# The squares of a conv norm, split in two fp32r parts and summed over channels by fp32r products

## The chip, the cores and the metric

The kernel runs on one core of one Trainium2 chip. The time is that of one execution on the device, in microseconds. It was 463.58 us as a median of three runs (463.23, 463.58 and 464.29).

## What is computed

One residual block of a streaming encoder: an RMSNorm, one input projection (1024 to 4096 columns), a gated linear recurrence (HGRN2, 4 heads of 128 channels) beside a gated short convolution over 512 channels, an output projection, the residual sum and a last RMSNorm. The part that matters here is the norm of the convolution's output, over 8 groups of 64 channels:

```python
def grouped_rmsnorm(x, g, n_groups):
    bsz, s, w = x.shape
    xf = x.astype(jnp.float32).reshape(bsz, s, n_groups, w // n_groups)
    y = xf * lax.rsqrt(jnp.mean(xf * xf, axis=-1, keepdims=True) + EPS)
    return (y.reshape(bsz, s, w) * g.astype(jnp.float32)).astype(x.dtype)
...
    y_b = gate_b * causal_depthwise_conv(gate_c * u, conv_w[l])
    o_b = grouped_rmsnorm(y_b, conv_norm_gain[l], CONV_GROUPS) * jax.nn.silu(z_b)
```

x has 1024 positions of 1024 channels, all in float32.

## The kernel before

Activations lie transposed: channels on the 128 partitions, positions along the free axis, in two halves (hf = 0 and 1) of W = 512 positions. A large product is made of two fp32r parts of each operand (a high part, which is the operand cast to fp32r, and a low part, which is what the cast lost): high by high, high by low and low by high, 128x512 each, on line 60. The cast is made on ACT (L314), the subtraction on DVE (L315).

The input projection goes through 14 pairs of column blocks in turn. Most pairs are seven products of 12 matmuls each, two early ones eight. While these stream through TensorE, the work on the results of earlier pairs is put between them. The order on each engine is the order in which the program writes the instructions; no scheduler moves them. The class Stream writes them: mm issues one large matmul and counts it; at(delay, ...) writes something that many matmuls later; later(delay, ...) does so for small jobs on TensorE, in the order in which they fall due, with at least 7 large matmuls between two of them. A job that is written a little later in the program can therefore change places with another.

The function conv_out(j) handles the convolution's output for channels j (four blocks of 128, so two norm groups each). For either half, on_b multiplies the result by its gate on DVE (L638), squares it on ACT (L639, into the tile b), and lets norm run 44 large matmuls after the bank's arrival (60 for j = 0). norm takes the mean over the 64 channels of a group with TensorE: four fp32 products, one for each 128 positions, with the squares as weights and bones, a 128x2 matrix with 1/64 in the rows of either group, as the moving operand. They go to the small tile pss in PSUM. ACT adds epsilon and moves them to r2 (L605), POOL takes the power -1/2 (L202), TensorE transposes r2 (prr), and the rows go through DRAM and come back spread over 64 partitions each (rs2), with which DVE scales the output (L629).

Three other things share the engines there. The recurrence of head j runs beside it: scores (tile psc: two small matmuls, emptied by ACT L481 and DVE L482) and combine (tile po, emptied by DVE L508 and ACT L510 and L511), as small jobs through the same later. All these small results (pss, prr, psc, po) use one pool of PSUM, psb, of two banks taken in turn, so each must wait until what was in its bank two jobs ago has been emptied. And POOL makes three multiplications for each half of the forget gate (L450, L451, L453), two for the gate of the convolution (L649, L650), and the powers. At the end of the projection POOL takes a power for head 3, scales vo (L543), and makes the last gates (L676), while DVE makes the low parts of the output weights (wol, L756).

Of the kernel before, what the change touches and what calls it, by code (L numbers as in the profile page):

```python
# [9 lines left out]
F32 = mybir.dt.float32  # L10
F32R = mybir.dt.float32r
I32 = mybir.dt.int32
AF = mybir.ActivationFunctionType
ALU = mybir.AluOpType
PSUM = bass.MemoryType.PSUM

P = 128
# [4 lines left out]
W = 512  # L22
NH = 4
# [65 lines left out]
def hybrid_block(ctx: ExitStack, tc: tile.TileContext, xT, x, wv, wpair, wout, cols, fgain, out):  # L89
    nc = tc.nc  # L90
    A, V, G, T = nc.scalar, nc.vector, nc.gpsimd, nc.tensor
# [5 lines left out]
    tmp = ctx.enter_context(tc.tile_pool(name="tmp", bufs=8))  # L97
    qk = ctx.enter_context(tc.tile_pool(name="qk", bufs=2))
    const = ctx.enter_context(tc.tile_pool(name="const", bufs=1))
# [3 lines left out]
    psb = ctx.enter_context(tc.tile_pool(name="psb", bufs=2, space=PSUM))  # L103
    pst = ctx.enter_context(tc.tile_pool(name="pst", bufs=2, space=PSUM))
    ctx.enter_context(tc.manual_schedule(engines={mybir.EngineType.PE, mybir.EngineType.SP, mybir.EngineType.Activation, mybir.EngineType.DVE, mybir.EngineType.Pool}))
    pe = Stream(nc)


    BUFS = {"tmp": 8, "keep": 3, "cn": 3}

    def t512(name, tag="tmp"):
        return tmp.tile([P, W], F32, tag=tag, name=name, bufs=BUFS[tag])

    def bank_a(i, name):
        return psa.tile([P, W], F32, tag=f"ps{i}", name=name)
# [1 line left out]
    def f32(ap):  # L117
        return ap.bitcast(F32)
# [12 lines left out]
    epsc = const.tile([P, 1], F32, name="epsc")  # L131
# [42 lines left out]
    def load_x(hf, k):  # L174
        if hf == 0:
            x0[k] = t512(f"x0_{k}")
        at = x_at(hf, k)
        hi, lo = v_parts(hf, k)
        g = col[:, C_NG + k:C_NG + k + 1]
        nc.sync.dma_start(at, xT[k, :, hf * W:(hf + 1) * W])  # L180
        if hf == 0 and k == 0:
            nc.sync.dma_start(col, cols)
        A.activation(hi, at, AF.Copy, scale=g)
        V.scalar_tensor_tensor(lo, at, g, f32(hi), op0=ALU.mult, op1=ALU.subtract)
# [10 lines left out]
    def half_row_sum(i):  # L195
        t, a = divmod(i, 2)
        xr = t512(f"xr{i}", "keep" if i < 3 else "cn") if i < 6 else qk.tile([P, W], F32, tag="kh", name=f"xr{i}")
        nc.sync.dma_start(xr, x[(4 + t) * P:(5 + t) * P, a * W:(a + 1) * W])
        A.activation(xr, xr, AF.Square, accum_out=(ssy if a else ssx[:, 1])[:, t:t + 1])

    def rsqrt(ap):
        G.tensor_tensor(ap, ap, mhalf[:, :ap.shape[1]], op=ALU.pow)  # L202
# [43 lines left out]
    def v_out(hf, t, p_):  # L246
# [3 lines left out]
    G.memset(mask, 1.0)  # L250
    G.affine_select(out=mask, in_=mask, pattern=[[1, P]], compare_op=ALU.is_ge, fill=0.0, base=0,
                    channel_multiplier=-1)
    bones = const.tile([P, 2], F32, name="bones")
    G.memset(bones, 0.0)
    G.memset(bones[0:64, 0:1], 1.0 / 64)
    G.memset(bones[64:128, 1:2], 1.0 / 64)
    for s_ in scbuf:
        G.memset(s_, 0.0)

# [13 lines left out]
        v_mms(0, pa, k)  # L273


    lbt = const.tile([P, 4, NH], F32, name="lbt")
    l0, l1 = col[:, C_HLB:C_HLB + NH], col[:, C_HLB + NH:C_HLB + 2 * NH]
    V.tensor_tensor(lbt[:, 0], l0, l1, op=ALU.max)
    V.tensor_tensor(lbt[:, 1], l0, lbt[:, 0], op=ALU.subtract)
# [77 lines left out]
    def keep(name, n, ps):  # L357
        kept[n, name] = t512(f"{name}_{n}", "keep")
        A.copy(kept[n, name], ps)
# [34 lines left out]
    def add(out_, ps, t):  # L394
        if t is None:
            A.copy(out_, ps)
        else:
            V.tensor_tensor(out_, ps, t, op=ALU.mult if t is rs1 else ALU.add)
# [150 lines left out]
    def conv_y(j, hf):  # L549
        return mb[:, j, hf * W:(hf + 1) * W]  # L550
# [44 lines left out]
    def conv_out(j):  # L595
        cg = col[:, C_CG + j:C_CG + j + 1]


        def norm(hf, sq):
            nm = f"{j}_{hf}"  # L600
            pss = psb.tile([P, 2, 4], F32, tag="ps", name=f"pss{nm}")
            for t in range(4):
                T.matmul(pss[:, :, t], sq[:, t * P:(t + 1) * P], bones, start=True, stop=True)
            r2 = sm.tile([P, 2, 4], F32, tag="r2", name=f"r2{nm}")
            pe.at(3, lambda: A.activation(r2, pss, AF.Identity, bias=epsc, scale=1.0))  # L605
            pe.at(10, lambda: rsqrt(r2.rearrange("p g t -> p (g t)")))

            def to_rows():
                prr = psb.tile([2 * 4, P], F32, tag="ps", name=f"prr{nm}")
                T.transpose(prr, r2.rearrange("p g t -> p (g t)"), ident)  # L610
                rr = sm.tile([2 * 4, P], F32, tag="rr", name=f"rr{nm}", bufs=1)
                pe.at(2, lambda: A.copy(rr, prr))
                pe.at(9, lambda: store(rr))

            def store(rr):
                rows = dram.tile([2 * 4, P], F32, tag="rows", name=f"rows{nm}")
                nc.sync.dma_start(rows, rr)
                pe.at(22, lambda: load(rows))

            def load(rows):  # L620
                rs2 = t512(f"rs2{nm}", "cn")
                for g in range(2):
                    nc.sync.dma_start(rs2[g * 64:(g + 1) * 64, :],
                                      rows[g * 4:(g + 1) * 4].rearrange("t p -> (t p)").partition_broadcast(64))
                pe.at(28, lambda: scale(rs2))

            def scale(rs2):
                y = conv_y(j, hf)
                V.scalar_tensor_tensor(y, y, cg, rs2, op0=ALU.mult, op1=ALU.mult)  # L629

            pe.later(28, to_rows)

        def on_b(hf):
            def on(ps, t):
                y = conv_y(j, hf)
                b = t512(f"b{j}_{hf}", "cn")
                add(b, ps, t)
                pe.at(4, lambda: V.tensor_tensor(y, y, b, op=ALU.mult))  # L638
                pe.at(14, lambda: A.activation(b, y, AF.Square))  # L639
                pe.later(60 if j == 0 else 44, lambda: norm(hf, b))  # L640
            return on

        def on_z(hf):
            def on(ps, t):
                y = conv_y(j, hf)
                z, sg = t512(f"z{j}_{hf}"), t512(f"sg{j}_{hf}")
                add(z, ps, t)
                pe.at(9, lambda: A.activation(sg, z, AF.Sigmoid))
                pe.at(14, lambda: G.tensor_tensor(z, z, sg, op=ALU.mult))  # L649
                pe.at(20, lambda: G.tensor_tensor(y, y, z, op=ALU.mult))  # L650
            return on

        return on_b(0), on_z(0), on_z(1), on_b(1)
# [109 lines left out]
    for g, (n, step) in enumerate(products):  # L763
        if n == npair - 1:
            i = ORDER.index(step)
# [62 lines left out]
    for i, (n, g) in enumerate(jobs):  # L828

        last = i == len(jobs) - 1  # L830
        for c0, c1 in [(0, W // 2), (W // 2, W)] if last else [(0, W)]:
            ps = []
# [21 lines left out]
        t = g[0]  # L854
# [74 lines left out]
```

## Time and profile before

| what | value |
|---|---|
| median of three runs | 463.58 us |
| the profiled execution | 464.61 us, of which 462.9 us are the span of the trace |
| TensorE (PE) | 454.9 us busy, 98% of the span |
| DVE | 326.1 us busy, 70% |
| ACT | 230.4 us busy, 50% |
| POOL | 101.3 us busy, 22% |
| mean granted clock of TensorE | 0.997 |

The span is the time that the profiler saw the engines at work; the device's time lies 1.7 us above it. A share of the busy time says how much an engine did, not whether the others waited for it; where one stands near 100%, only its own work and its waits count.

### The profile page before, as it was taken

What the parts mean: (1) busy time and instruction counts of PE and PEld (TensorE: products, weight loads), DVE (VectorE), ACT (ScalarE), POOL (GpSimd) and SP (SyncE); (2) the same over time, 40 slices, a digit from 0 to 9 for tenths busy, and PEclk for the clock granted to TensorE, in tenths of its full rate; (3) what the DMA queues carried; (4) which work ended last, traced back from release to release, by engine and by line L of the source; (5) the groups of instructions that cost most, each with busy time, mean ns of one, the idle gap of its engine ahead of it and who ended that gap; (6) DMA issues with size and microseconds to landing.
All of it is one profiled execution on the core that took longest, in us unless ns stands there. A gap on an engine that the chain in (4) does not pass through costs nothing. (4 is left out here: it accounts for less than half of the span.)

```text
span 462.9 us, 6245 instructions
## 1 busy us (share of the span) xinstructions
PE 454.9 (98%) x2200; PEld 380.5 (82%) x2200; DVE 326.1 (70%) x593; ACT 230.4 (50%) x553; POOL 101.3 (22%) x92
## 2 busy tenths in 40 slices
PE   8999999999999999999999999999999999999995
PEld 6888888888888887888888888888888888888884
DVE  3658787989977789658799468798466795523333
ACT  5877416474454554454443545454636734314333
POOL 1100000005520053410326210326332443220000
PEclk9999999999999999999999999999999999999998
DMA  8990311020022120022020212020014238101442
GB/s 265 396 380 6 92 45 47 23 68 25 23 92 92 24 68 25 23 92 91 24 69 24 66 49 92 23 90 26 24 33 144 75 101 274 57 2 70 161 157 91
DMA packets 22031, 40.83 MB, mean 88 GB/s; under 512 B 2736, under 2 KB 2800, under 8 KB 22000
## 3 DMA queue, kind: packets, MB, share of 16 engines
q1 hardware_dynamic: 22000, 40.43, 26.3%
q8 instruction: 17, 0.28, 0.2%
q14 instruction: 14, 0.11, 0.1%
HBM read 36.19 MB, written 4.23 MB: 87 GB/s over the span
## 5 line engine op out<-in xcount | busy, mean ns | idle before, releaser
L315 DVE TENSOR_TENSOR lT<-T,hT 128x512 fp32r<-128x512 f32 x48 | 32.5, 678 | 32.4 <-ACT hT L314 32.2
L450 POOL TENSOR_TENSOR kh<-kh,ei 128x512 f32<-128x512 f32 x8 | 11.7, 1465 | 136.5 <-DVE ei L449 136.5
L60 PE MATMUL pb<-XH,lT 128*128 128x512 f32 x96 | 38.9, 405 | 0.0
L60 PE MATMUL pb<-XL,hT 128*128 128x512 f32 x96 | 38.4, 400 | 0.0
L60 PE MATMUL pb<-XH,hT 128*128 128x512 f32 x96 | 37.7, 393 | 0.0
L510 ACT COPY vo<-po 128x128 f32<-128x128 f32 x32 | 8.5, 266 | 53.9 <-DVE st L508 40.4
L314 ACT CAST hB<-B 128x512 fp32r<-128x512 f32 x44 | 27.6, 629 | 10.7 <-issue 10.7
L60 PE MATMUL po<-XH,XL 128*128 128x512 f32 (+1 forms) x88 | 32.6, 371 | 0.0
L60 PE MATMUL po<-XH 128*128 128x512 f32 (+1 forms) x88 | 32.6, 371 | 0.0
L60 PE MATMUL po<-XL,XH 128*128 128x512 f32 (+1 forms) x88 | 32.6, 370 | 0.0
L315 DVE TENSOR_TENSOR lB<-B,hB 128x512 fp32r<-128x512 f32 x44 | 32.3, 733 | 0.2 <-ACT hB L314 0.2
L314 ACT CAST hT<-T 128x512 fp32r<-128x512 f32 x48 | 28.4, 591 | 4.2 <-DVE T L306 4.2
L449 DVE RECIPROCAL ei<-e 128x128 f32<-128x128 f32 x32 | 29.5, 932 | 0.0
L60 PE MATMUL p<-XH,hB 128*128 128x512 f32 x64 | 24.9, 389 | 0.0
L60 PE MATMUL p<-XL,hB 128*128 128x512 f32 x64 | 24.9, 389 | 0.0
L60 PE MATMUL p<-XH,lB 128*128 128x512 f32 x64 | 24.9, 389 | 0.0
L482 DVE COPY_PREDICATED sc<-mask,psc 128x128 f32<-128x128 int32 x32 | 9.6, 300 | 16.7 <-ACT kt L481 16.6
L60 PEld LDWEIGHTS pb<-XL,hT 128*128 128x128 f32 x96 | 18.0, 188 | 4.1
L60 PEld LDWEIGHTS pb<-XH,hT 128*128 128x128 f32 x96 | 18.0, 188 | 3.7
L60 PEld LDWEIGHTS pb<-XH,lT 128*128 128x128 f32 x96 | 18.1, 189 | 3.0
L845 DVE TENSOR_TENSOR r<-po,xo 128x512 f32<-128x512 f32 (+1 forms) x9 | 5.7, 633 | 19.9 <-PE po L60 19.9
L60 PE MATMUL pe<-XL,hT 128*128 128x512 f32 x48 | 19.5, 405 | 0.0
(217 smaller groups left out, 1364.2 us busy)
## 6 DMA issues: line engine op xcount, KB each, us to landing
B<-wpair SPq DMA_DIRECT2D x56, 256.0 KB, 2.7
wo<-wout SPq DMA_DIRECT2D x16, 256.0 KB, 3.0
xo<-x SPq DMA_DIRECT2D x16, 256.0 KB, 3.3
out<-y SPq DMA_DIRECT2D x16, 256.0 KB, 2.3
wv<-wv SPq DMA_DIRECT2D x8, 256.0 KB, 7.5
x<-xT SPq DMA_DIRECT2D x8, 256.0 KB, 5.8
vo<-x SPq DMA_DIRECT2D x4, 512.0 KB
mb<-xT SPq DMA_DIRECT2D x8, 256.0 KB, 6.0
```

The costliest lines, as they stand in the source:

```text
L60: self.T.matmul(*args, **kw)
L314: A.copy(hi, src)
L315: pe.at(5, lambda: V.tensor_tensor(lo, src, f32(hi), op=ALU.subtract))
L449: pe.at(9 + gap * i, lambda c0=i * P: V.reciprocal(eis[0][:, c0:c0 + P], e[:, c0:c0 + P]))
L450: pe.at(10 + 4 * gap - 3, lambda: G.tensor_tensor(kh, kh, eis[0], op=ALU.mult), lambda: G.tensor_tensor(ev[:, :, 0, :], ev[:, :, 0, :], ei ...
L482: lambda: V.copy_predicated(scbuf[(h * NT + pr) % NS], mask.bitcast(I32), psc[:, 0]))
L510: A.copy(vp, po[:, 0])
L845: V.tensor_tensor(r, po[:, c0:c1], xr[:, c0:c1], op=ALU.add)
```

## The change

The squares b are no longer used as fp32. Behind the square ACT casts them to fp32r (sh, the high part), and five large matmuls later in the program DVE subtracts this from b (sl, the low part, rounded to fp32r). bones becomes fp32r (its values 0 and 1/64 are exact), made from a small fp32 tile. norm multiplies either part by bones and sums them in PSUM: eight fp32r products in place of four fp32 ones. pss changes its layout, so that the two columns of a product lie side by side, and r2 is written through a rearranged view. norm comes 4 large matmuls later than before. sh and sl are two more tiles of the ring tmp, of 8 buffers.

```diff
-    bones = const.tile([P, 2], F32, name="bones")
-    G.memset(bones, 0.0)
-    G.memset(bones[0:64, 0:1], 1.0 / 64)
-    G.memset(bones[64:128, 1:2], 1.0 / 64)
+    bones = const.tile([P, 2], F32R, name="bones")
+    lbt = const.tile([P, 4, NH], F32, name="lbt")
+    ones2 = lbt[:, 3, 0:2]
+    G.memset(ones2, 0.0)
+    G.memset(ones2[0:64, 0:1], 1.0 / 64)
+    G.memset(ones2[64:128, 1:2], 1.0 / 64)
+    V.tensor_copy(bones, ones2)
...
-        def norm(hf, sq):
+        def norm(hf, parts):
             nm = f"{j}_{hf}"
-            pss = psb.tile([P, 2, 4], F32, tag="ps", name=f"pss{nm}")
+            pss = psb.tile([P, 4, 2], F32, tag="ps", name=f"pss{nm}")
             for t in range(4):
-                T.matmul(pss[:, :, t], sq[:, t * P:(t + 1) * P], bones, start=True, stop=True)
+                for i, sq in enumerate(parts):
+                    T.matmul(pss[:, t], sq[:, t * P:(t + 1) * P], bones, start=(i == 0), stop=(i == 1))
             r2 = sm.tile([P, 2, 4], F32, tag="r2", name=f"r2{nm}")
-            pe.at(3, lambda: A.activation(r2, pss, AF.Identity, bias=epsc, scale=1.0))
+            pe.at(3, lambda: A.activation(r2.rearrange("p g t -> p t g"), pss, AF.Identity, bias=epsc, scale=1.0))
...
                 pe.at(4, lambda: V.tensor_tensor(y, y, b, op=ALU.mult))
-                pe.at(14, lambda: A.activation(b, y, AF.Square))
-                pe.later(60 if j == 0 else 44, lambda: norm(hf, b))
+                parts = []
+
+                def square():
+                    A.activation(b, y, AF.Square)
+                    parts.extend([t512(f"s{i}{j}_{hf}", dtype=F32R) for i in "hl"])
+                    A.copy(parts[0], b)
+                    pe.at(5, lambda: V.tensor_tensor(parts[1], b, f32(parts[0]), op=ALU.subtract))
+
+                pe.at(14, square)
+                pe.later(64 if j == 0 else 48, lambda: norm(hf, parts))
```

What this does to the order of the instructions is seen at four places. In these rows a name is that of a tile with a running number, which differs between the two programs, and the line numbers of the changed kernel are higher by 2 to 11.

On DVE, at the first norm (j = 0, hf = 0), before the change: the multiplication by the gate (L638), the last of the four reciprocals, and the low parts of the next two weights.

```order
L638 TENSOR_TENSOR mb<-mb,b_0_983 128x512
L449 RECIPROCAL ei_0_966<-e_0_942 128x128
L315 TENSOR_TENSOR lT_3_1011<-T_3_985,hT_3_1010 128x512
L315 TENSOR_TENSOR lB_3_1018<-B_3_861,hB_3_1017 128x512
L398 TENSOR_TENSOR z_0_1030<-pd_923,u_2_1005 128x512
```

And with it:

```order
L641 TENSOR_TENSOR mb<-mb,b_0_984 128x512
L451 RECIPROCAL ei_0_967<-e_0_943 128x128
L648 TENSOR_TENSOR sl_0_1012<-b_0_984,sh_0_1011 128x512
L317 TENSOR_TENSOR lT_3_1015<-T_3_986,hT_3_1014 128x512
L317 TENSOR_TENSOR lB_3_1022<-B_3_862,hB_3_1021 128x512
L400 TENSOR_TENSOR z_0_1035<-pd_924,u_2_1006 128x512
```

The subtraction stands between the reciprocal and the low parts, which move behind it.

On ACT, at the second square of j = 0 (b_1), which is also where r2 of the first norm is made, before:

```order
L359 COPY m_3_1122<-pb_1094 128x512
L639 ACTIVATE b_1_1092<-mb 128x512
L314 CAST hT_3_1131<-T_3_1095 128x512
L605 ACTIVATE r_0_1121<-pss_0_1116,epsc 128x8
L359 COPY m_3_1155<-pd_1124 128x512
L314 CAST hT_3_1160<-T_3_1125 128x512
```

And with the change:

```order
L361 COPY m_3_1121<-pb_1099 128x512
L645 ACTIVATE b_1_1097<-mb 128x512
L647 CAST sh_1_1130<-b_1_1097 128x512
L316 CAST hT_3_1133<-T_3_1100 128x512
L608 ACTIVATE r_0_1149<-pss_0_1140,epsc 128x4x2
L361 COPY m_3_1167<-pd_1123 128x512
L316 CAST hT_3_1172<-T_3_1124 128x512
```

The cast sh_1 stands between the square and what came after it; r2 keeps its place among the others.

On TensorE, at the first norm of j = 1, before: the norm (pss_0), seven large matmuls, and the first combine of head 1 (po_0).

```order
L60 MATMUL pb_1590<-XL,hT_5_1652 128x512
L603 MATMUL pss_0_1779<-bones,b_0_1676 128x2 x4
L60 MATMUL pb_1590<-XH,lT_5_1653 128x512
...
L60 MATMUL pb_1796<-XH,lB_6_1664 128x512
L492 MATMUL po_0_1802<-vo,kt_0_1730 128x128
L495 MATMUL po_0_1802<-vo,sc_97 128x128
```

And with the change:

```order
L60 MATMUL pb_1607<-XH,hT_5_1668 128x512
L494 MATMUL po_0_1802<-vo,kt_0_1751 128x128
L497 MATMUL po_0_1802<-vo,sc_97 128x128
L60 MATMUL pb_1607<-XL,hT_5_1668 128x512
...
L60 MATMUL pb_1818<-XL,hB_6_1680 128x512
L606 MATMUL pss_0_1829<-bones,sh_0_1717 128x2
L606 MATMUL pss_0_1829<-bones,sl_0_1718 128x2
```

The two have changed places; j = 2 and j = 3 do the same, j = 0 doesn't (there the norm and everything small behind it come 4 large matmuls later, but for the two scores products after the norm).

On ACT, at the end of the projection, before: the last result of head 3 (po_7) is copied to vo and squared, and then a bank is copied (m_13).

```order
L510 COPY vo<-po_7_3595 128x128
L511 ACTIVATE po_7_3595,ssa<-po_7_3595 128x128
L359 COPY m_13_3602<-pe_3579 128x512
L755 CAST woh_3573<-wo_7_3575 128x512
L755 CAST XH<-wo_2_3577 128x512
L538 ACTIVATE ssa<-ssa,epsc 128x8
```

And with the change:

```order
L361 COPY m_13_3665<-pe_3644 128x512
L512 COPY vo<-po_7_3661 128x128
L513 ACTIVATE po_7_3661,ssa<-po_7_3661 128x128
L766 CAST woh_3638<-wo_7_3640 128x512
L766 CAST XH<-wo_2_3642 128x512
L540 ACTIVATE ssa<-ssa,epsc 128x8
```

The copy m_13 stands ahead of the two on po_7. On POOL the second scaling of vo then comes after the last two gates instead of before them.

## Rows read from the trace of the kernel before

**Rows 1.** Windows: busy us and instructions of PE, PEld, DVE, ACT, POOL; clock.

```profile
core 0: us, PE busy (x) PEld busy (x) DVE busy (x) ACT busy (x) POOL busy (x), PEclk, DMA share, GB/s
100.00:380.00 280.00, 279.69 (x1412) 234.54 (x1411) 221.09 (x411) 143.20 (x380) 86.25 (x68) 1.00 0.19 59
111.20:120.30 9.10, 9.10 (x45) 7.65 (x44) 9.10 (x17) 4.22 (x9) 5.15 (x5) 1.00 0.00 0
```

**Rows 2.** Timeline of PE at the first norm: start, duration, instruction, idle before.

```profile
117.11 0.39 PE L60 MATMUL pb<-XH,lB 128*128 128x512 f32 x1
117.34 0.95 PE L603 MATMUL pss<-bones,b 128*128 128x2 f32 x8
118.14 0.49 PE L60 MATMUL pd<-XH,hT 128*128 128x512 f32 x1
118.47 0.40 PE L60 MATMUL pd<-XL,hT 128*128 128x512 f32 x1
```

**Rows 3.** Groups of instructions, line 603, TensorE: busy us, mean ns, idle before.

```profile
L603 PE MATMUL pss<-bones,b 128*128 128x2 f32 x64 | 7.7, 242 | 0.3 <-DVE sc L482 0.3
```

**Rows 4.** Timelines of PE and DVE at the first norm of j = 1.

```profile
181.68 0.39 PE L60 MATMUL pb<-XL,hT 128*128 128x512 f32 x1
182.37 1.05 PE L603 MATMUL pss<-bones,b 128*128 128x2 f32 x8 [0.31 <-DVE sc L482]
...
182.02 0.65 DVE L482 COPY_PREDICATED sc<-mask,psc 128x128 f32<-128x128 int32 x2
```

**Rows 5.** Timeline of PE, the last two products of 256 columns.

```profile
456.74 0.28 PE L60 MATMUL po<-XL,XH 128*128 128x256 f32 x1
456.86 0.28 PE L60 MATMUL po<-XH,XL 128*128 128x256 f32 x1
```

**Rows 6.** Groups of instructions, by form: a cast, a subtraction.

```profile
L315 DVE TENSOR_TENSOR lB<-B,hB 128x512 fp32r<-128x512 f32 x44 | 32.3, 733 | 0.2 <-ACT hB L314 0.2
...
L314 ACT CAST hB<-B 128x512 fp32r<-128x512 f32 x44 | 27.6, 629 | 10.7 <-issue 10.7
```

**Rows 7.** Timelines of POOL and DVE, j = 0.

```profile
109.33 1.29 POOL L450 TENSOR_TENSOR kh<-kh,ei 128x512 f32<-128x512 f32 x1 [67.10 <-DVE ei L449]
111.61 0.61 POOL L453 TENSOR_TENSOR kh<-kh,gt 128x256 f32<-128x256 f32 x1
...
110.11 1.06 DVE L315 TENSOR_TENSOR lB<-B,hB 128x512 fp32r<-128x512 f32 x1
120.35 0.62 DVE L638 TENSOR_TENSOR mb<-mb,b 128x512 f32<-128x512 f32 x1
```

**Rows 8.** Timeline of ACT, j = 0: both squares, and r2 of the first norm.

```profile
108.36 0.63 ACT L639 ACTIVATE b<-mb 128x512 f32<-128x512 f32 x1 [1.12 <-DVE mb L638]
...
121.01 0.63 ACT L639 ACTIVATE b<-mb 128x512 f32<-128x512 f32 x1 [1.50 <-DVE mb L638]
...
122.01 0.27 ACT L605 ACTIVATE r<-pss,epsc 128x8 f32<-128x8 f32 x1
```

**Rows 9.** Timeline of PE, the second scores product of head 0.

```profile
123.19 0.38 PE L478 MATMUL psc<-qh,kh 128*128 128x128 f32 x2
```

**Rows 10.** Timelines of POOL, DVE and PE around the second square of j = 1.

```profile
191.09 1.29 POOL L650 TENSOR_TENSOR mb<-mb,z 128x512 f32<-128x512 f32 x1 [0.23 <-POOL z L649]
...
192.07 0.34 DVE L508 SCALAR_TENSOR_TENSOR st<-po,gg,dec 128x128 f32<-128x128 f32 x1
...
193.48 0.39 PE L478 MATMUL psc<-qh,kh 128*128 128x128 f32 x2
```

**Rows 11.** Timelines of ACT, POOL, DVE and PE at the output projection's start.

```profile
365.07 0.59 ACT L359 COPY m<-pe 128x512 f32<-128x512 f32 x1
...
366.97 2.02 POOL L202 TENSOR_TENSOR ssa<-ssa,mhalf 128x8 f32<-128x8 f32 x1 [1.45 <-ACT ssa L538]
...
371.52 3.43 POOL L676 TENSOR_TENSOR za<-za,sga 128x512 f32<-128x512 f32 x2
...
373.74 1.77 DVE L756 TENSOR_TENSOR wol<-wo,woh 128x512 fp32r<-128x512 f32 x1
...
375.59 0.47 PE L60 MATMUL po<-wol,XH 128*128 128x512 f32 x1
```

More of the change, by code (lines that the diff above doesn't have):

```diff
@@ L109, in hybrid_block, with t512 @@
     BUFS = {"tmp": 8, "keep": 3, "cn": 3}
-    def t512(name, tag="tmp"):
-        return tmp.tile([P, W], F32, tag=tag, name=name, bufs=BUFS[tag])
+    def t512(name, tag="tmp", dtype=F32):
+        return tmp.tile([P, W], dtype, tag=tag, name=name, bufs=BUFS[tag])
     def bank_a(i, name):
@@ L273, in hybrid_block @@
         v_mms(0, pa, k)
-    lbt = const.tile([P, 4, NH], F32, name="lbt")
     l0, l1 = col[:, C_HLB:C_HLB + NH], col[:, C_HLB + NH:C_HLB + 2 * NH]
```

## The prediction

> **What bounds the kernel now.** I read the windows first, because they say which engine the end of the program hangs on. In the stretch from 100 to 380 us, where all the squares and norms lie, TensorE is busy 279.69 of 280.00 us, at a granted clock of 1.00 (the upper of the two levels, 2.4 GHz) [rows 1]. Nothing that DVE, ACT or POOL do costs time there unless TensorE must wait for it. So the change is worth two things: the difference in TensorE's own work, and the stalls that it makes or removes. The second number of [rows 1] matters as much: from 111.2 to 120.3 us DVE is busy 9.10 of 9.10 us. There a DVE operation more moves all DVE work behind it.
>
> Next, the timeline of TensorE around one norm, for its price. The products of 128x512 start 0.23 us apart (the last one ahead of the norm at 117.11, the norm at 117.34); the norm's four fp32 products stand as eight passes, from 117.34 to 118.14, that is 0.80 us or 0.10 each, and the fp32r product after them has its successor 0.33 later (118.47) instead of 0.23 [rows 2]. With those 0.10 the norm takes 0.90 us of TensorE's time, 0.112 per pass. For the whole kernel the grouped line has 64 passes for 8 norms of 4 products, so one fp32 product is two passes [rows 3].
>
> Last, I went along TensorE's timeline for places where it does wait. There is one of weight: at 182.37, after the product of 181.68, so 0.69 us later instead of 0.23; the row names DVE's L482, whose two copies run from 182.02 for 0.65 us [rows 4]. They empty the psb bank that the norm wants.
>
> **TensorE's own work.** Removed: 32 fp32 products, 64 passes [rows 3]. Added: 64 fp32r products of the same 128 columns of weights and the same 2 moving columns. No row shows an fp32r product of 2 columns, so I bound it. Two columns by themselves are nothing (0.23 us for 512 columns is 0.001 for two), so what a pass costs is its weights. An fp32r load of 128 columns that isn't hidden costs the 0.10 us by which the product after the norm is late [rows 2]: 64 x (0.10 - 0.112) = -0.8 us. From above, fp32r products of 256 columns start 0.12 us apart [rows 5]: 64 x (0.12 - 0.112) = +0.5. Both ends say that one load is paid per pass, and there are 64 before and after. I take 0.112, a change of 0.
>
> A page of the Trainium skill speaks to this: FP8 and Floating Point Precision, section TensorE Precision Notes, says that true FP32 takes four passes. By it the old norms would be 128 passes, 64 more than the new ones, worth an estimated 64 x 0.112 = 7.2 us. The trace counts two per product, so I don't follow it.
>
> **DVE's and ACT's added work.** Per norm, ACT makes one cast from fp32 to fp32r and DVE one subtraction, both 128x512. The same forms take 0.629 and 0.733 us on the mean [rows 6]; in a row of such work the next one starts some 0.55 us (ACT) and 0.6 us (DVE) later. 8 x 0.6 = 5 us on either engine, which is free as long as it isn't late for TensorE.
>
> It becomes dear where POOL works at the same time. The trace shows it at 110.11: DVE's lB<-B,hB, both operands in SBUF, takes 1.06 us instead of some 0.65, and ends at 111.17; POOL's L450 ran from 109.33 to 110.62 [rows 7]. It ends 0.55 us after POOL is done, as if it had begun only then. The Trainium skill gives a rule for it (SBUF — State Buffer, section Who interferes with whom): a DVE instruction with two SBUF inputs and a GpSimd instruction that reads SBUF exclude each other. The trace agrees with 1.06 us, and it speaks against this change, whose subtraction is of that kind.
>
> **First term, j = 0 (109 to 125 us).** sh_0 stands on ACT right after the square that starts at 108.36 and lasts 0.63 [rows 8]; it ends at about 109.6. The subtraction sl_0 stands on DVE before lT and lB, so it starts inside POOL's L450 and takes over lB's fate: it ends at about 111.17. Then lT, and lB starts at about 111.7, where POOL's L453 runs from 111.61 to 112.22 [rows 7]: lB ends at 112.77 instead of 111.17. DVE is 1.6 us late (1.15 if lB comes first; 0.6 to 0.7 if POOL doesn't get in the way), and without a gap up to 120.3 [rows 1] it stays late until the multiplication L638 of hf = 1, 120.35 in the trace [rows 7]. Its square starts at 121.01 + 1.6 = 122.6; behind it ACT has sh_1 (+0.55), a cast, and then r2 of hf = 0, now done at 122.28 [rows 8]: at 122.28 + 1.6 + 0.55 = 124.4. That r2 empties the bank that the second scores product takes at 123.19 [rows 9]. TensorE is there no later than before, so it waits about 124.4 + 0.1 - 123.2 = 1.3 us. Bounds: with DVE late by 0.65 it waits 0.4; if the blocking goes further, 1.9. I take 1.3.
>
> **Second term, j = 1.** The norm's delay of 48 lets the first combine (po1_0) go ahead of the norm, so po1_0 now wants the bank that L482 empties, at the product where the norm wanted it. The subtraction sl stands ahead of L482 on DVE: 182.67 + 0.7 = 183.4 at most, and DVE can make up some 0.3 to 0.4 by its pauses; the stall of 0.46 [rows 4] grows by about 0.25 (0 to 0.7). For hf = 1, sl_1 would run at about 191.5, inside POOL's L650 (191.09 to 192.38), and ends at 192.9; lT and the state update of 192.07 come after it, so at about 193.6, and ACT's square that empties po1_1 half a microsecond behind at 194.4. The norm's transposes prr want that bank just after the scores of 193.48, at about 194.2 [rows 10]. With the next combine waiting for the state: +0.4 (0 to 0.8). Together +0.65.
>
> **Third term, j = 2 and 3.** The same swap of norm and combine, with the same extra DVE operation, in a stretch with less DVE work. I take +0.1 each (0 to 0.3).
>
> **Fourth term, the start of the output projection.** At 375.59 the product takes wol<-wo, which DVE finishes at 375.51 (L756, 373.74 and 1.77 us: blocked by POOL's L676, two from 371.52 for 3.43, end 374.95, plus 0.55). That POOL chain begins with the pow at 366.97, which waited for ACT [rows 11]. In the changed kernel ACT has the bank copy m (0.59 us, [rows 11]) ahead of the last copy and square of po3_7, so the sum for head 3 comes 0.45 us later, and one step after another so do the pow, the scalings, the gates and wol. TensorE has no slack there: +0.4 (0 to 0.5).
>
> **What costs nothing.** The fp32r ones are made by POOL and DVE before the first product needs DVE. The 16 tiles more in the tmp ring are each free well before they are wanted. ACT's r2 writes the same 8 values per partition in another order. The row loads from DRAM move behind a few weight fetches on SP's queue, but the scaling that waits for them comes some 10 us later; if that cover were gone, the put of the output projection would be late, far behind.
>
> **Sum.** 0 + 1.3 + 0.65 + 0.2 + 0.4 = +2.6 us. The profiled execution took 464.61 us, 1.0 above the median of 463.58 (span 462.9), so by its own time 467.2; against the median 466.2.
>
> **The rivals.** Hidden (chance 0.21): POOL doesn't block sl_0, and DVE's lateness is eaten by pauses and by operations that wait for POOL in any case. Then j = 0 gives 0.4, the rest 0 to 0.4: 463.6 to 464.4. For it: an operation blocked already loses nothing by coming later; against it: [rows 1] has no gap in DVE. Below 464.5 it counts as no change.
>
> Faster (0.06): an fp32r load hides behind the pass before it where an fp32 one doesn't, so a pass costs far less. At half, 64 x 0.056 = 3.6 us saved, 463.58 - 3.6 + 2.6 = 462.6; fully hidden 7.2, so 459.0, or 456.4 without stalls. It decides once a pass costs under about 0.06 us. Against it: the 0.10 of the fp32r product behind the norm [rows 2] is just such a load, not hidden. A third of this chance (0.02) is for old products of four passes each, of which the trace records two: then 64 passes of 128 fall away, again 64 x 0.112 = 7.2 us, 459.0 with the stalls. That is what the rule of four passes (the Trainium skill, FP8 and Floating Point Precision, TensorE Precision Notes) would do here; 64 rows for 32 products [rows 3] speak against it.
>
> Worse (0.08): j = 2 and 3 stall like j = 1, and the blocking in j = 0 goes one operation further: 1.9 + 1.3 + 1.0 + 0.5 = 4.7, 468.3.
>
> **How the numbers follow.** The forecast, slower by the four stalls, has 0.65: 464.6 to 467.6 by its bounds. With the hidden rival's upper part the range is 463.6 to 467.6; it leaves out 0.06 (faster), the worst case of 0.08 and little else. A difference of 0.2% (0.93 us, about as much as the three runs differ) can't be told from none: faster 0.06, same 0.21, slower 0.73.
>
> **What the changed profile would show.** Right: L606 with 64 rows some 0.1 us apart; sl_0 of j = 0 at about 109.6 with 1.5 us; r2 of hf = 0 at about 124; a gap on TensorE before the second scores product of over 1 us, one before po1_0 of 0.5 to 0.9, one of 0.3 to 0.5 at the first wol1. Wrong: no gap before 125 us (then the cover held), or norms that take half of 0.90 us (then the load was hidden). TensorE's busy time should not change by over 0.8 us.

## The result: 1.3% slower, with most of the stalls where the prediction took almost none

The changed kernel takes 469.73 us (median; 469.43 to 470.87), the kernel before 463.4 us beside it: a ratio of 1.0125, 95% interval 1.0101 to 1.0148. The forecast was 466.2 us, 463.6 to 467.6. The direction was right; the size, 2.6 us, was well under half of the 6.3 us that came.

TensorE has the same work and more waits. The windows of the changed kernel give the stretch in which [rows 1] showed 279.69 us busy of 280:

```profile
core 0: us, PE busy (x) PEld busy (x) DVE busy (x) ACT busy (x) POOL busy (x), PEclk, DMA share, GB/s
100.00:380.00 280.00, 276.04 (x1383) 229.24 (x1381) 228.69 (x411) 145.74 (x382) 89.06 (x68) 1.00 0.17 54
```

To see where they lie, I set the start of each 128x512 product of line 60 in one trace against that of the same product in the trace of before, and took the growth of the difference over each stage (products 440 to 700 hold the norms of j = 0, 700 to 800 and 940 to 1070 and 1200 to 1340 those of j = 1, 2 and 3, 1400 to 1460 the first output weights; elsewhere it is 0.05 or less). That leaves the first microseconds out, and they must be left out: in the profiled execution of the changed kernel TensorE is 1.26 us early already at the 20th product, so its span is 4.8 us longer (467.7 against 462.9) where the loss behind that product is 6.1.

| us lost by TensorE | j = 0 | j = 1 | j = 2 | j = 3 | output | all |
|---|---|---|---|---|---|---|
| predicted | 1.3 | 0.65 | 0.1 | 0.1 | 0.4 | 2.6 |
| changed kernel | 1.53 | 0.40 | 1.81 | 1.88 | 0.45 | 6.1 |

The price of a pass was right. The timeline of TensorE at the first norm, which answers to [rows 2]:

```profile
116.76 0.39 PE L60 MATMUL pd<-XH,hT 128*128 128x512 f32 x1
116.99 0.17 PE L606 MATMUL pss<-bones,sh 128*128 128x2 f32 x1
117.02 0.25 PE L606 MATMUL pss<-bones,sl 128*128 128x2 f32 x1
117.13 0.25 PE L606 MATMUL pss<-bones,sh 128*128 128x2 f32 x1
...
117.69 0.25 PE L606 MATMUL pss<-bones,sl 128*128 128x2 f32 x1
117.80 0.49 PE L60 MATMUL pd<-XL,hT 128*128 128x512 f32 x1
118.12 0.40 PE L60 MATMUL pd<-XH,lT 128*128 128x512 f32 x1
```

There are eight passes, the first two 0.03 us apart and the others 0.11. From the first to the product behind them it is 0.81 us, and 0.32 for that product: the 0.80 and 0.33 of before.

At j = 0 the chain came as forecast. The timelines of POOL, DVE, ACT and TensorE, for [rows 7 to 9]:

```profile
108.07 1.30 POOL L452 TENSOR_TENSOR kh<-kh,ei 128x512 f32<-128x512 f32 x1 [67.11 <-DVE ei L451]
...
108.42 1.49 DVE L648 TENSOR_TENSOR sl<-b,sh 128x512 fp32r<-128x512 f32 x1 [0.50 <-ACT sh L647]
...
120.70 0.66 DVE L641 TENSOR_TENSOR mb<-mb,b 128x512 f32<-128x512 f32 x1
...
123.11 0.28 ACT L608 ACTIVATE r<-pss,epsc 128x8 f32<-128x8 f32 x1
...
121.69 0.39 PE L60 MATMUL pa<-XL,hB 128*128 128x512 f32 x1
123.44 0.49 PE L480 MATMUL psc<-qh,kh 128*128 128x128 f32 x2 [1.36 <-ACT r L608]
```

sl_0 takes 1.49 us inside POOL's L452 and ends 0.54 us after it; the multiplication of the next half starts at 120.70, which with the head start of 1.26 is 1.61 us later than in [rows 7] (forecast: 1.6); r2 is done at 123.39, and the scores product waits for it.

The large losses are at j = 2 and 3, with three stalls each. The same engines at j = 2:

```profile
253.33 1.62 POOL L661 TENSOR_TENSOR mb<-mb,z 128x512 f32<-128x512 f32 x1
257.05 1.29 POOL L660 TENSOR_TENSOR z<-z,sg 128x512 f32<-128x512 f32 x1 [2.10 <-ACT sg L659]
...
260.35 1.27 POOL L661 TENSOR_TENSOR mb<-mb,z 128x512 f32<-128x512 f32 x1
...
253.73 1.24 DVE L501 TENSOR_TENSOR gg<-gt 128x3 f32<-128x3 f32 x1
255.08 0.35 DVE L508 TENSOR_SCALAR st<-po,gg 128x128 f32<-128x128 f32 x1
...
257.13 1.75 DVE L641 TENSOR_TENSOR mb<-mb,b 128x512 f32<-128x512 f32 x1
...
260.94 0.30 DVE L484 COPY_PREDICATED sc<-mask,psc 128x128 f32<-128x128 int32 x1 [1.45 <-ACT kt L483]
261.15 1.01 DVE L648 TENSOR_TENSOR sl<-b,sh 128x512 fp32r<-128x512 f32 x1
262.09 0.68 DVE L317 TENSOR_TENSOR lT<-T,hT 128x512 fp32r<-128x512 f32 x1
262.69 0.33 DVE L510 SCALAR_TENSOR_TENSOR st<-po,gg,dec 128x128 f32<-128x128 f32 x1
...
255.82 0.19 ACT L513 ACTIVATION_READ_ACCUMULATOR po<-po 128x1 f32 x1
...
258.92 0.63 ACT L645 ACTIVATE b<-mb 128x512 f32<-128x512 f32 x1 [1.47 <-DVE mb L641]
259.64 0.62 ACT L647 CAST sh<-b 128x512 fp32r<-128x512 f32 x1
...
256.06 0.49 PE L480 MATMUL psc<-qh,kh 128*128 128x128 f32 x2 [0.33 <-DVE z L400]
...
261.30 0.49 PE L480 MATMUL psc<-qh,kh 128*128 128x128 f32 x2 [0.52 <-DVE sc L484]
...
263.70 0.27 PE L613 MATMUL prr<-ident,r 128*8 128x128 f32 x1 [0.18 <-issue]
```

Three DVE operations with both operands in SBUF start while a POOL multiplication of 128x512 runs, and each ends after it: gg (three columns) takes 1.24 us, the multiplication L641 takes 1.75, sl_1 takes 1.01. In the trace of before gg takes 0.15 and the multiplication 0.68. POOL isn't idle there either, but it runs the power L202, of 8 columns, and neither of them is held by that:

```profile
253.24 1.63 POOL L202 TENSOR_TENSOR r<-r,mhalf 128x8 f32<-128x8 f32 x1
...
253.84 0.68 DVE L638 TENSOR_TENSOR mb<-mb,b 128x512 f32<-128x512 f32 x1
254.44 0.15 DVE L499 TENSOR_TENSOR gg<-gt 128x3 f32<-128x3 f32 x1
```

In the changed kernel each of the three holds the bank that the next small job on TensorE wants. gg holds the state update st, and behind that ACT's copies of po, the last of which ends at 256.01; the scores product comes at 256.06 (the row names DVE's z, which that product doesn't read). L641 holds ACT's square, and behind it the casts sh and hT and the copy of kt, for which L484 waited; the product follows at 261.30. sl_1 holds the second st and ACT's copies; prr comes at 263.70.

The output projection starts as forecast: wol ends at 380.31 and TensorE takes it at 380.37, 0.63 after the product before.

```profile
379.74 0.39 PE L60 MATMUL po<-woh,XH 128*128 128x512 f32 x1
380.37 0.50 PE L60 MATMUL po<-wol,XH 128*128 128x512 f32 x1 [0.24 <-DVE wol L767]
...
378.79 1.52 DVE L767 TENSOR_TENSOR wol<-wo,woh 128x512 fp32r<-128x512 f32 x1
```

### The profile page after: what moved, and what is told of

Its sections match the earlier page's. It is cut to its first block, busy times and chain, and to the rows that moved or that the text cites. A ratio compares the mean times of both kernels' runs of the same rounds, so it can differ in the third digit from the quotient of the medians.

```text
span 467.7 us, 6246 instructions
## 1 busy us (share of the span) xinstructions
PE 455.7 (97%) x2200; PEld 378.4 (81%) x2200; DVE 339.6 (73%) x602; ACT 235.9 (50%) x561; POOL 104.1 (22%) x92
## 5 line engine op out<-in xcount | busy, mean ns | idle before, releaser
L452 POOL TENSOR_TENSOR kh<-kh,ei 128x512 f32<-128x512 f32 x8 | 11.7, 1468 | 132.5 <-DVE ei L451 120.3
L316 ACT CAST hB<-B 128x512 fp32r<-128x512 f32 x44 | 27.6, 629 | 10.7 <-issue 10.7
L484 DVE COPY_PREDICATED sc<-mask,psc 128x128 f32<-128x128 int32 x32 | 9.5, 298 | 23.1 <-ACT kt L483 23.0
L202 POOL TENSOR_TENSOR r<-r,mhalf 128x8 f32<-128x8 f32 x8 | 15.3, 1912 | 24.6 <-ACT r L608 24.6
```

What stands on the lines that cost most here:

```text
L316: A.copy(hi, src)
L452: pe.at(10 + 4 * gap - 3, lambda: G.tensor_tensor(kh, kh, eis[0], op=ALU.mult), lambda: G.tensor_tensor(ev[:, :, 0, :], ev[:, :, 0, :], ei ...
L484: lambda: V.copy_predicated(scbuf[(h * NT + pr) % NS], mask.bitcast(I32), psc[:, 0]))
```

## The experiments

Two theories stood at first. Theory 1: the new order does it, since norm and combine have changed places at j = 1 to 3. Theory 2: DVE and ACT have one operation more per norm and are late, whatever the order. The runs have their rows in the table at the end of this section. The kernel before, run beside them, had medians of 464.4, 464.67 and 463.45 us in the three groups of runs, so I go by ratios and by TensorE's loss.

**e1_order_back** keeps the split and gives the norm its old place:

```diff
-                pe.later(64 if j == 0 else 48, lambda: norm(hf, parts))
+                pe.later(60 if j == 0 else 44, lambda: norm(hf, parts))
```

> The changed kernel with the norm's old delays (44, and 60 for j = 0), so that norm and combine stand on TensorE in the order of before; the split and the eight fp32r products stay. Theory 1 (order): most of j = 2 and j = 3 (1.8 us each in the changed kernel) comes from the swap of norm and combine, which moves the gate product gg and the state update on DVE to a place where POOL works; then j = 2 and 3 lose at most 0.3 us each here, the output projection about 0, j = 0 still 1.5, j = 1 0.2 to 0.7: 465.2 to 466.0 us. Theory 2 (load): DVE and ACT have one operation more per norm and are late whatever the order; then j = 2 and 3 still lose 1.2 us or more each: 468 us or more.

Measured: 471.94 us, a ratio of 1.0137 (1.0088 to 1.0187), TensorE 6.4 us late: 1.93, 1.80, 1.41 and 1.13 at the four norms, 0 at the output projection. Theory 1 is wrong on the norms and right on the output projection; the 1.2 us or more of theory 2 came at j = 2 and nearly at j = 3. In the old order gg isn't held (0.15 us), but sl_1 is; at j = 2:

```profile
263.19 1.30 POOL L661 TENSOR_TENSOR mb<-mb,z 128x512 f32<-128x512 f32 x1 [0.23 <-POOL z L660]
...
263.80 1.24 DVE L648 TENSOR_TENSOR sl<-b,sh 128x512 fp32r<-128x512 f32 x1 [0.93 <-ACT sh L647]
...
265.56 0.34 DVE L510 SCALAR_TENSOR_TENSOR st<-po,gg,dec 128x128 f32<-128x128 f32 x1
...
266.53 0.49 PE L480 MATMUL psc<-qh,kh 128*128 128x128 f32 x2 [0.80 <-ACT po L513]
```

One held operation ahead of st, and the scores product waits for po's bank.

**e2_order_only** gives the kernel before the new delays and nothing else:

```diff
-                pe.later(60 if j == 0 else 44, lambda: norm(hf, b))
+                pe.later(64 if j == 0 else 48, lambda: norm(hf, b))
```

> The kernel before with the norm's new delays (48, and 64 for j = 0), fp32 products and no split. Theory 1 (order): j = 2 and 3 lose 1.0 to 1.8 us each by the new order alone, the output projection 0.4, j = 0 nothing, j = 1 gains its old stall of 0.46 and loses as much: 466 to 467.5 us. Theory 2 (load): no stall in j = 2 and 3 over 0.3 us; 463.0 to 464.0 us.

Measured: a ratio of 0.9982 (0.996 to 1.0004). The order alone costs 0 at j = 2 and 3, as theory 2 had it. It wins 0.56 at j = 1, which is the old stall of [rows 4]: the large products around that norm stand 1.61 us apart, those around the other norms 1.04. And it costs 0.43 at the output projection. And yet gg and L638 are held here just as long as in the changed kernel:

```profile
250.00 1.60 POOL L650 TENSOR_TENSOR mb<-mb,z 128x512 f32<-128x512 f32 x1
...
250.39 1.23 DVE L499 TENSOR_TENSOR gg<-gt 128x3 f32<-128x3 f32 x1
...
253.78 1.76 DVE L638 TENSOR_TENSOR mb<-mb,b 128x512 f32<-128x512 f32 x1
...
253.34 0.39 PE L478 MATMUL psc<-qh,kh 128*128 128x128 f32 x2
```

The difference is when. Here gg starts 2.95 us ahead of the scores product, in the changed kernel 1.8 ahead of when it was due (256.06 less the stall of 0.50, less 253.73). In the changed kernel it is 2.33 us from gg's start (253.73) to the product that takes the freed bank (256.06), 1.1 of them the lock. That fits into 2.95 and not into 1.83; the 0.50 by which it doesn't is the stall.

**e3_no_sl** leaves out the subtraction and uses sh twice:

```diff
-                    parts.extend([t512(f"s{i}{j}_{hf}", dtype=F32R) for i in "hl"])
+                    parts.extend([t512(f"sh{j}_{hf}", dtype=F32R)] * 2)
                     A.copy(parts[0], b)
-                    pe.at(5, lambda: V.tensor_tensor(parts[1], b, f32(parts[0]), op=ALU.subtract))
```

> The changed kernel without the subtraction on DVE: the second product of each pair takes sh again, so the output leaves out the low part and counts the high part twice. The cast on ACT and the new order stay. Theory 1 (order): j = 0 loses under 0.5 us (no operation there any more that POOL can block), j = 2 and 3 still 1.0 us or more each: 465.5 to 467.5 us. Theory 2 (load): the DVE operation is the cause everywhere, 463.5 to 464.5 us.

Measured: 2.6 us of loss (0.47, -0.23, 1.14, 0.82 and 0.41), a ratio of 1.0057 (1.0033 to 1.0081). Without any subtraction more than half of j = 2 is still there: the cast alone, in the new order, is enough to be late. At j = 2 gg starts 2.0 us ahead of when the scores product is due, the product comes 2.33 us after it again (252.91 and 255.24), and that is 0.32 late. So neither theory is whole.

**e4_gg_early** is the changed kernel with one tiny operation moved:

```diff
                   lambda: V.copy_predicated(scbuf[(h * NT + pr) % NS], mask.bitcast(I32), psc[:, 0]))
+            if pr == 0:
+                pe.at(2, lambda: V.tensor_tensor(gg[:, 0:3], gts[:, 0:3, 1], gts[:, 1:4, 0], op=ALU.mult))
...
-                if pr == 0:
-                    V.tensor_tensor(gg[:, 0:3], gts[:, 0:3, 1], gts[:, 1:4, 0], op=ALU.mult)
```

> The changed kernel with the small gate product gg of the first half made right after the first scores' copy on DVE in place of ahead of the first state update. If the first link of the chain in j = 2 and 3 is gg, held by POOL's L661 for 1.1 us there (1.24 us in the changed kernel, 0.15 in the kernel before), then the first of the three stalls in j = 2 and in j = 3 (0.50 and 0.57 us) goes, and the blocked multiplication L641 behind it may too: 466.5 to 468.8 us. If gg is only where the blocking shows and another operation takes its place, the loss stays at 1.5 us or more each: 469 to 470 us.

Measured: the loss falls from 6.1 to 2.1 us, j = 2 and 3 from 1.81 and 1.88 to 0.48 and 0.18, more than expected; a ratio of 1.0025 (1.0005 to 1.0046). At its new place gg takes 0.45 us, and the later links hold no one up for long, though L641 and sl are held as before (1055 and 948 ns on the mean).

**e5_j0_late** moves one subtraction past POOL's work:

```diff
-                    pe.at(5, lambda: V.tensor_tensor(parts[1], b, f32(parts[0]), op=ALU.subtract))
+                    pe.at(30 if j == 0 and hf == 0 else 5, lambda: V.tensor_tensor(parts[1], b, f32(parts[0]), op=ALU.subtract))
```

> The changed kernel with one subtraction moved: sl_0 of j = 0, hf = 0 is written 30 large matmuls after the cast in place of 5, past POOL's five multiplications; everything else stays, so DVE does the same work. Theory 1 (POOL's lock): the j = 0 loss of 1.54 us falls to 0.3 to 0.7 us, what 0.6 us of DVE and 0.55 us of ACT leave beyond the slack of 0.9; the other stages stay as in the changed kernel. Theory 2 (mere load): DVE is as full as before, the loss at j = 0 stays at 1.2 to 1.6 us.

Measured: j = 0 loses 1.10 us in place of 1.53, between both expectations, and the rest stays; the ratio is 1.0099 (1.0065 to 1.0132). The reason for the miss is in DVE's next row:

```profile
108.34 0.69 DVE L317 TENSOR_TENSOR lT<-T,hT 128x512 fp32r<-128x512 f32 x1 [0.98 <-ACT hT L316]
```

In the trace of before this lT waited 0.32 us for ACT's hT; now sh stands ahead of hT and lT waits 0.98. The cast alone makes DVE late by 0.58 (the start of L641 in e3_no_sl, 120.73, plus that trace's head start of 0.20, less 120.35); the subtraction itself adds 0.6 (119.71 + 1.82 in this run, 1.18 late); the rest of the 1.61, 0.43, goes with sl_0's place inside POOL's work.

**e8_no_gate** takes POOL's L661 away:

```diff
                 pe.at(14, lambda: G.tensor_tensor(z, z, sg, op=ALU.mult))
-                pe.at(20, lambda: G.tensor_tensor(y, y, z, op=ALU.mult))
```

> The changed kernel without POOL's L661, the multiplication of the convolution's output by its gate (the output leaves that factor out); DVE, ACT and TensorE keep all their work and order. Theory 1 (POOL's lock): gg takes 0.15 us and sl_1 0.7, and j = 2 and j = 3, 1.8 us each in the changed kernel, lose 0 to 0.7 us each. Theory 2 (mere load of DVE and ACT): each loses 1.2 us or more still.

Measured: j = 2 and 3 lose 0.38 and 0.08, as theory 1 (here POOL's lock) had it; all stages lose 0.84, a ratio of 1.001 (0.9988 to 1.0031). The same place as above:

```profile
253.54 0.15 DVE L501 TENSOR_TENSOR gg<-gt 128x3 f32<-128x3 f32 x1
253.79 0.35 DVE L508 TENSOR_SCALAR st<-po,gg 128x128 f32<-128x128 f32 x1
...
259.88 0.68 DVE L648 TENSOR_TENSOR sl<-b,sh 128x512 fp32r<-128x512 f32 x1
...
255.39 0.39 PE L480 MATMUL psc<-qh,kh 128*128 128x128 f32 x2
```

gg starts as late as in the changed kernel (1.85 us ahead of the scores product) and takes 0.15 us; sl_1 takes 0.68. DVE and ACT do all their work, late as it is, and TensorE doesn't wait for gg. It still waits a little behind L641, which L660 holds as before (1.76 us). At j = 0 the run says less: sl_0 is held as before (1.49 us), but three scans of DVE behind it take 1.74 us in place of the 2.79 of both kernels, since no L661 runs beside them, and DVE makes up 1 us there.

**e6_best** keeps the split and moves its work: gg early, and

```diff
-                    A.copy(parts[0], b)
-                    pe.at(5, lambda: V.tensor_tensor(parts[1], b, f32(parts[0]), op=ALU.subtract))
+                    hi, lo = parts
+                    pe.at({(0, 0): 6, (0, 1): 5}.get((j, hf), 5 if hf else 0), lambda: A.copy(hi, b))
+                    pe.at({(0, 0): 30, (0, 1): 18}.get((j, hf), 18 if hf else 5),
+                          lambda: V.tensor_tensor(lo, b, f32(hi), op=ALU.subtract))
...
-                pe.later(64 if j == 0 else 48, lambda: norm(hf, parts))
+                pe.later(64 if j == 0 else 44 if j == 3 else 48, lambda: norm(hf, parts))
```

> The changed kernel with its split and its eight products, and the new work put elsewhere: gg early, sl_0 of j = 0 30 later, casts and subtractions of hf = 1 behind the next head work (5 and 18 large matmuls later in place of 0 and 5), and the old delay of 44 for j = 3, for the order at the output projection. If only the places of the new work cost time, TensorE's loss falls from 6.1 us to 0 to 1.0: 463.2 to 464.6 us, no better than before, since a pass costs the same. If the work itself costs, it stays at 3 us or more: above 466 us.

Measured: 0.16 us of loss in all, a ratio of 0.9996 (0.9975 to 1.0017). The same operations, well placed, cost nothing, and they win nothing.

**e7_one_part** drops the low part, and with it half of the passes; bones, pss and r2 are as in the changed kernel:

```diff
...
-                pe.at(14, lambda: A.activation(b, y, AF.Square))
-                pe.later(60 if j == 0 else 44, lambda: norm(hf, b))
+                sq = []
+
+                def square():
+                    sq.append(t512(f"sh{j}_{hf}", dtype=F32R))
+                    A.activation(sq[0], y, AF.Square)
+
+                pe.at(14, square)
+                pe.later(60 if j == 0 else 44, lambda: norm(hf, sq[0]))
```

> The kernel before with the squares written by ACT straight as fp32r (the high part alone, rounded; the low part is left out), and four fp32r products per norm: no cast, no subtraction, the old delays. If a pass costs 0.112 us whether fp32 or fp32r, 32 passes of 64 go: 3.6 us less, 459.3 to 460.3 us. If an fp32r product of this shape cost as much as an fp32 one of two passes, the time would be that of before, 463 to 464 us.

Measured: a ratio of 0.9926 (0.9899 to 0.9953). Its group of norm products, with half the count of [rows 3]:

```profile
L605 PE MATMUL pss<-bones,sh 128*128 128x2 f32 x32 | 4.1, 233 | 0.3 <-DVE sc L484 0.3
```

j = 2 and 3 win 0.89 us each: 8 passes less at 0.112 are 0.90. j = 0 wins only 0.53 (a new wait of 0.35 before prr), so all is 3.1 in place of 3.6. **e7_again** is the same kernel once more.

> The same kernel as e7_one_part, beside the run above on the same chip: 0.992 to 0.994 of the time of before, TensorE ends 3.1 us earlier.

It gave 0.9927 (0.9905 to 0.9949). Beside it ran **e9_one_part_48**, the one part with gg early and the norms' delays at 60, 48, 48 and 44.

> One fp32r part (the low part is left out) with four products per norm, as in e7_one_part, now with gg early and the norm's delays 60, 48, 48 and 44. If the stall of 0.46 us at the norm of j = 1 is only a matter of the norm's place, it goes here (the changed kernel with gg early gained 0.56 at j = 1), and TensorE ends 3.6 us or more before the kernel before, 0.5 earlier than e7_one_part: 0.991 of the time of before or less. If another job takes the stall over in j = 1 or j = 2, it stays at 3.1 us as in e7_one_part.

Measured: the stall of j = 1 is gone and TensorE ends 3.7 us earlier than before, as expected. The ratio, 0.9933 (0.9913 to 0.9953), can't be told from the one above, and the 0.991 that was expected lies just below its interval. Either beats both kernels, at the price of rounding the squares to fp32r.

Each row below is one execution against that of before. e7_one_part and e7_again, one kernel twice, differ by 0.02 us at most in a stage.

| us lost by TensorE | j = 0 | j = 1 | j = 2 | j = 3 | output | all |
|---|---|---|---|---|---|---|
| changed kernel | 1.53 | 0.40 | 1.81 | 1.88 | 0.45 | 6.1 |
| e1_order_back | 1.93 | 1.80 | 1.41 | 1.13 | -0.01 | 6.4 |
| e2_order_only | -0.10 | -0.56 | 0.00 | 0.00 | 0.43 | -0.2 |
| e3_no_sl | 0.47 | -0.23 | 1.14 | 0.82 | 0.41 | 2.6 |
| e4_gg_early | 1.53 | -0.56 | 0.48 | 0.18 | 0.46 | 2.1 |
| e5_j0_late | 1.10 | 0.39 | 1.80 | 1.84 | 0.46 | 5.6 |
| e8_no_gate | 0.48 | -0.56 | 0.38 | 0.08 | 0.46 | 0.8 |
| e6_best | 0.36 | -0.56 | 0.11 | 0.26 | -0.01 | 0.2 |
| e7_one_part | -0.53 | -0.78 | -0.89 | -0.89 | 0.00 | -3.1 |
| e7_again | -0.55 | -0.80 | -0.89 | -0.89 | -0.01 | -3.1 |
| e9_one_part_48 | -0.56 | -1.37 | -0.89 | -0.91 | -0.01 | -3.7 |

## Why the prediction was wrong

**TensorE's own work: right.** 0.112 us per pass held for fp32r (0.11 apart in the changed kernel; 0.89 us for 8 passes less in e7_one_part). So the change takes nothing from TensorE, and all of it is loss.

**The first term: right, with one of its causes missed.** 1.3 was forecast and 1.53 came; DVE was late by 1.61 us, for which 1.6 was worked out. The working put 1.0 of it on POOL and forgot that lT waits for ACT, where the cast now stands ahead. The runs give 0.58 to the cast, 0.6 to the subtraction and 0.43 to POOL, so that 1.6 came out is luck: one cause was missed and another taken too large. ACT's part was too small as well: the cast waits for the square, so r2 is 0.7 and not 0.55 behind.

**The second term: near by luck.** 0.65 was forecast and 0.40 came, but only hf = 1 came as told: 0.35 at prr and 0.09 at the combine behind it, for 0.4. The stall of [rows 4] didn't grow, and po1_0 didn't wait: the stall went, as it goes with the new order alone (-0.56 in e2_order_only). And 0.52 came at the second scores product, behind L641, which POOL holds there too (1.75 us at 187.94); the working didn't have that.

**The third term is the step that failed:** "The same swap of norm and combine, with the same extra DVE operation, in a stretch with less DVE work. I take +0.1 each (0 to 0.3)." It measured 1.81 and 1.88, 3.5 us more than taken, which is all of the miss. No row stood behind the 0.1, and its reason doesn't hold: in the trace of before DVE is busy for 8.54 of the 8.70 us from 246.9 to 255.6, no less than at j = 1 (8.84 of 9.00 from 180 to 189). I had weighed POOL's lock for the new subtraction alone, and at j = 2 and 3 not even for that: in e1_order_back, where gg isn't held, sl_1 is, and they still lose 1.41 and 1.13. The swap also moves old operations: gg and the multiplication L641 now start inside POOL's L661 and L660, and the trace of before, in which gg took 0.15 us, doesn't show that. What the runs show in its place is that two things must meet. The lock of gg and L638 without the lateness costs 0 (e2_order_only); the lateness without POOL's L661 costs 0.38 and 0.08 (e8_no_gate); together they cost 1.8. The Trainium skill (SBUF — State Buffer, section Who interferes with whom) says that a DVE instruction with two SBUF inputs contends with a GpSimd instruction that reads SBUF. That fits each of the held rows, and the smallest best: gg has three columns and stands 1.24 us. It doesn't fit POOL's power L202, whose operands are in SBUF too: in the trace of before gg and L638 run inside it in 0.15 and 0.68 us, and there the measurement decides.

**The fourth term: right** (0.4 was forecast, 0.45 came). It belongs to the order: 0.43 in e2_order_only, 0 where j = 3 has its old delay.

**The rivals.** Hidden: wrong as forecast, though e6_best shows that it was to be had. Faster: wrong; passes cost the same. Worse: the nearest, with its stalls at j = 2 and 3 and 4.7 us; it had 0.08, and its 468.3 us are still too few. The range was also narrower than the bounds of its own terms, which add up to 0.4 and 4.5 us, so 464.0 and 468.1 us in place of 464.6 and 467.6; the result lies outside either.

What isn't settled is how the loss of one stage divides among its three stalls: with gg moved (e4_gg_early) the second went too, and the third shrank at j = 3 and not at j = 2, so they aren't independent.

## What to carry to other kernels

When a change moves work on an engine that isn't the bound, look up what each moved operation will meet at its new place, old ones and tiny ones too, and how long before its result is wanted it starts; a hold of 1.1 us is free with 2.95 us of room and dear with 1.8. Where two products take the place of one, count passes, not products: fp32 was two passes here, so two fp32r parts win nothing and only dropping a part does. And an added cast delays what stands behind it on its engine, and with it the engine that waits for that: here 0.58 us of DVE for a cast on ACT.

## What wasn't expected of the hardware

A DVE operation of 128x3 elements takes as long as POOL's multiplication lasts, 1.24 us for 0.15, when both its operands are in SBUF. One operand in PSUM is enough for it not to be held: L484, which reads the scores from PSUM, takes its 0.30 us at 260.94, inside POOL's L661 of 260.35 to 261.62. And in the kernel before the subtraction for lT, whose T lies in PSUM (the pool pst), takes 0.70 us inside the L450 of [rows 7] that holds the one for lB, with both operands in SBUF, to 1.06:

```profile
109.50 0.70 DVE L315 TENSOR_TENSOR lT<-T,hT 128x512 fp32r<-128x512 f32 x1 [0.32 <-ACT hT L314]
```

POOL is held as well: its L453 of 128x256, 0.62 us at 108.76 in e5_j0_late, takes 1.08 in the changed kernel, where it starts at 109.32 and sl_0 runs to 109.91.

The first products of line 60 run at different speeds from one execution to the next. Of the kernel before, and then of the changed one:

```profile
7.18 0.63 PE L60 MATMUL pv<-XH 128*128 128x512 f32 x1
7.61 0.63 PE L60 MATMUL pv<-XL,XH 128*128 128x512 f32 x1
```

```profile
7.14 0.40 PE L60 MATMUL pv<-XH,XL 128*128 128x512 f32 x1
7.38 0.39 PE L60 MATMUL pv<-XH 128*128 128x512 f32 x1
```

They are 0.43 us apart in the one and 0.24 in the other; before's are so until 9.3 us, and most of the 1.26 us of head start comes from that. These are the spacings of the two levels of TensorE's clock: in e1_order_back the granted clock is 0.50 from 7.5 to 10.7 us (1.2 GHz), with products 0.43 apart, and 1.00 from 11 us on (2.4 GHz), with 0.23. In the trace of before the view gives 1.00 for the first microseconds too, so there it is the spacing alone that shows the lower level. In all three traces sixteen small products and a wait of 0.97 to 1.68 us for the first operand come before. Why one execution stays at the lower level longer than another is not shown. The times of one kernel differ by as much as this and more: 469.43 to 470.87 us for the changed one, 462.68 to 467.23 for the kernel before in the largest group of runs.
